# Low parts of the weights by negation and an accumulating DMA, with four buffers

## The chip, the cores and the metric

The kernel runs on one core of one Trainium2 chip. Its time is device microseconds (us) of the whole program. Names of the engines: PE is TensorE (matmuls; its weight loads are PEld), DVE is VectorE, ACT is ScalarE, POOL is GpSimd, SP is SyncE, which here issues most of the DMAs. L254 is line 254 of the kernel file.

## The reference

A trunk of two decoder layers over 512 tokens of width 1024 in float32. Per layer, with all products in full precision:

```
h = RMSNorm(x);  z = h @ W_in           # 5888 columns: attention q,k,v; retention q,k,v,g; two gates
A = sliding-window attention (window 128, 8 query and 2 key heads of 64, rotary, sinks)
B = retention (4 heads, 128 and 256 wide), normed per head, times silu(g)
y = sigmoid(gate_a) * (A @ W_a) + sigmoid(gate_b) * (B @ W_b)
x = x + y @ W_out                        # up to here: "the mixer"
x = x + relu(RMSNorm(x) @ W_up)^2 @ W_down   # "the MLP", 4096 wide
```

A last RMSNorm ends it.

## The kernel before

**Full precision out of three products.** PE multiplies in a float32 form with a shortened mantissa (float32r). Each operand is therefore split in two parts: the high part is the operand rounded to that form, the low part is what the rounding left over. A product is then high x high + high x low + low x high. These are the three matmuls of `products` on L299, L300 and L301; in the wide pairs of the MLP the two lines L1155 and L1156 do the same on 512 and 256 columns.

**Weight units.** The weights lie in HBM cut into units of 128 partitions x 1024 words (512 KB), in the order in which they are used. A layer's mixer has 66: 46 of w_in, 4 of w_a, 8 of w_b and 8 of w_out, with the w_a and w_b units standing between those of w_in. The MLP's units (w_up, w_down, and "pair" units that are sums of weight blocks) follow. `order` holds this list for both layers.

**Load, split, use.** Three functions move along that list, each with its own counter:

- `load_until` lets SP load a unit into a raw tile (L194); there are three raw tiles.
- `split_until(n)` splits all units before n: ACT rounds the raw tile into `hi` (L253; for the first half unit DVE does, L251), and DVE subtracts `hi` from the raw tile into `lo` (L254). Before each unit it calls `load_until(i + 3)`. The tiles `hi` and `lo` come from `wpool`, three buffers each, so the high part of a unit waits until PE is done with the unit three before it. The first three units are split in two halves, to start early.
- `unit` hands the next unit to PE's code and has the units up to two further on split ahead (`split_until(i + 3)`).

In the MLP `add_part` has DVE add or subtract weight blocks ahead of the split; the last units of all go to other tiles (`homes`).

**Users.** `group` uses four units for four 128-column outputs at once (five PSUM banks serve all of this), `chunk` one unit for one output of 128 columns, with two steps of background work (`advance`) between; `values` uses four units as the moving operand. A unit of the mixer is eight blocks of 128x128 and so 24 matmuls of 512 columns. Attention and retention are generators whose matmuls are put between those of the chunks.

**Order.** The order of the instructions on each engine comes from a scheduler that plans the program ahead with times of its own; each engine then runs its list strictly in order and waits where an operand isn't there. POOL has almost nothing to do before the change: constants and a few memsets at the start, one memset per layer (L545), and one scaling at the end (L506).

Of the kernel before, what the change touches and what calls it, by code (L numbers as in the profile page):

```python
# [12 lines left out]
F32R = mybir.dt.float32r  # L13
AF = mybir.ActivationFunctionType
ALU = mybir.AluOpType
# [3 lines left out]
P = 128  # L19
# [26 lines left out]
UNIT = 1024  # L46
# [9 lines left out]
def unit_order():  # L56

    order = [("w_in", i) for i in range(4 + 2 + 8 + 2 + 4 + 2)]
    order += [("w_in", i) for i in range(22, 26)]
    order += [("w_a", i) for i in range(4)]  # L60
    order += [("w_in", i) for i in range(26, 42)]
    order += [("w_b", i) for i in range(4)]
    order += [("w_in", i) for i in range(42, 46)]
    order += [("w_b", i) for i in range(4, 8)]
    order += [("w_out", i) for i in range(8)]
    for what, q, i in mlp_sequence():
        if what == "first":
            order += [("w_up", u) for u in range(4)]
        elif what == "pair":
            order += [("pair", 8 * q + 2 * i, part) for part in range(4)]  # L70
        elif what == "down":
            order += [("w_down", 8 * q + 2 * i + u) for u in range(2)]
        else:
            order += [("w_down", 8 * q + u) for u in range(8)]
    return order
# [13 lines left out]
def wide(chunk):  # L89

    return FIRST_WIDE <= chunk < LAST_WIDE
# [32 lines left out]
def decoder(ctx, tc, xT, x_first, w_in, w_a, w_b, w_out, w_up, w_down, tables, decay, band, triangles, g_last, out):  # L124
    nc = tc.nc
    weights = {"w_in": w_in, "w_a": w_a, "w_b": w_b, "w_out": w_out, "w_up": w_up, "w_down": w_down}

    const = ctx.enter_context(tc.tile_pool(name="const", bufs=1))
    wpool = ctx.enter_context(tc.tile_pool(name="wpool", bufs=3))
# [6 lines left out]
    def f32(ap):  # L136
        return ap.bitcast(F32)
# [26 lines left out]
    order = [(layer, *u) for layer in range(DEPTH) for u in unit_order()]  # L164
    raws, parts, homes = {}, {}, []
    state = {"next": 0, "loaded": 0, "split": 0}

    def halves(i):

        return (slice(0, UNIT // 2), slice(UNIT // 2, UNIT)) if i < 3 else (slice(0, UNIT),)  # L170

    last_low = []
# [11 lines left out]
    def load_until(n):  # L184
        while state["loaded"] < min(n, len(order)):
            i = state["loaded"]
            layer, name, j = order[i][:3]
            if name == "pair":
                load_part(i)
            else:  # L190
                raws[i] = raw_tile()
                for at in halves(i):
                    queue = nc.scalar if i == 0 and at.start == 0 else nc.sync
                    queue.dma_start(raws[i][:, at], weights[name][layer, j][:, at])  # L194
                    if i < 3:
                        load_x()
            state["loaded"] += 1
# [17 lines left out]
    def add_part(i):  # L215
        part = order[i][3]
        if part == 0:
            w2 = raws[i + 3]
            nc.vector.tensor_tensor(raws[i][:, RIGHT], w2[:, RIGHT], w2[:, LEFT], ALU.add)
        elif part == 1:  # L220
            w1 = raws[i - 1]
            nc.vector.tensor_tensor(raws[i][:, LEFT], w1[:, RIGHT], w1[:, LEFT], ALU.subtract)
        elif part == 2:
            raws[i] = big("raw3").rearrange("p a t -> p (a t)")
            w1, w2, z2 = raws[i - 2], raws[i + 1], raws[i - 1]
            nc.vector.tensor_tensor(raws[i][:, LEFT], w1[:, LEFT], w2[:, RIGHT], ALU.subtract)
            nc.vector.tensor_tensor(raws[i][:, RIGHT], z2[:, RIGHT], z2[:, LEFT], ALU.subtract)

    def split_until(n):
        while state["split"] < min(n, len(order)):  # L230
            i = state["split"]
            load_until(i + 3)
            paired = order[i][1] == "pair"
            if paired:
                add_part(i)
            raw = raws[i]
            if homes and i >= len(order) - len(homes):
                home = homes[len(order) - 1 - i]
                hi, lo = (home[:, 2 * a : 2 * a + 2, :].rearrange("p a t -> p (a t)") for a in range(2))
            else:  # L240


                first = (ASIDE, ASIDE) if paired else (0, 0)
                if paired and wide(order[i][2]):
                    first = (ASIDE, 0)
                hi, lo = (
                    wpool.tile([P, UNIT + P], F32R, tag=n, name=n)[:, a : a + UNIT] for n, a in zip(("hi", "lo"), first)
                )
            for at in (LEFT,) if paired and order[i][3] == 3 else halves(i):
                if i == 0 and at.start == 0:  # L250
                    nc.vector.tensor_copy(hi[:, at], raw[:, at])  # L251
                else:
                    nc.scalar.activation(hi[:, at], raw[:, at], AF.Copy)  # L253
                last_low[:] = [nc.vector.tensor_tensor(lo[:, at], raw[:, at], f32(hi[:, at]), ALU.subtract).ins]  # L254
            raws.pop(i - 3 if paired else i, None)
            parts[i] = (hi, lo)
            state["split"] += 1

    def unit(name, layer):
        i = state["next"]  # L260
        assert order[i][:2] == (layer, name), (order[i], layer, name)
        state["next"] += 1
        split_until(i + 3)
        return parts.pop(i)


# [66 lines left out]
    def chunk(name, layer, moving, evacuate, rate=1.0):  # L333

        hi, lo = unit(name, layer)
        n = len(moving)
        ps = bank(ps_mm, "mm")
        pairs = [((hi[:, k * P : (k + 1) * P], lo[:, k * P : (k + 1) * P]), moving[k]) for k in range(n)]
        advance(rate)
        products(ps, pairs[: n // 2], True, False)  # L340
        advance(rate)
        products(ps, pairs[n // 2 :], False, True)
        evacuate(ps)

    def group(name, layer, moving, evacuates, meanwhile=None):


        banks = [bank(ps_mm, "mm") for _ in range(4)]
        for u in range(4):
            hi, lo = unit(name, layer)  # L350
            for j in range(2):
                k = 2 * u + j
                for c, ps in enumerate(banks):
                    cols = slice(j * T + c * P, j * T + (c + 1) * P)
                    products(ps, [((hi[:, cols], lo[:, cols]), moving[k])], k == 0, k == KD - 1)
            if meanwhile and u in meanwhile:
                meanwhile[u]()
        return [partial(evacuate, ps) for ps, evacuate in zip(banks, evacuates)]
# [5 lines left out]
    def two_chunks(name, layer, moving, evacuates):  # L364

        banks = [bank(ps_mm, "mm") for _ in range(2)]
        for u in range(2):
            hi, lo = unit(name, layer)
            for j in range(4):
                k = 4 * u + j  # L370
                for c, ps in enumerate(banks):
                    cols = slice((2 * j + c) * P, (2 * j + c + 1) * P)
                    products(ps, [((hi[:, cols], lo[:, cols]), moving[k])], k == 0, k == KD - 1)
        for ps, evacuate in zip(banks, evacuates):
            evacuate(ps)
# [58 lines left out]
    def end(layer, uT):  # L434
# [24 lines left out]
        for u in range(4):  # L459
            weights = unit("w_down", layer)  # L460
            split_until(state["next"] + 2 + u)
            for j in range(2):
                k = 2 * u + j
                for b, ps in enumerate(banks):
                    multiply(ps, k, b, weights, k == 0, k == KD - 1)
# [803 lines left out]

    scaled_input(0, 0)  # L1270
    split_until(1)
    for u in (2, 3):
        for k in (2 * u - 3, 2 * u - 2):
# [160 lines left out]
```

## Time and profile before

| | |
|---|---|
| median of 3 runs | 1481.8 us (1481.06 to 1482.15) |
| span of the profiled execution, first to last instruction | 1480.1 us |
| the profiled execution's own time | not listed apart; the median of the runs lies 1.7 us above the span |
| DMA | 155.57 MB moved, 147.51 MB read from HBM |

The page of the profile gives busy time per engine, its share in 40 slices of the span, the DMA queues, the chain of work that ended last, and groups of equal instructions by line. A group names what is written and read (`lo<-raw,hi`), the shape, the count, the busy time in us and the mean of one in ns, and then the idle time ahead of these instructions with what ended it. A PE row's length is that of one matmul from start to end; matmuls overlap, so the pace is the distance between two starts.

### The profile page before, as it was taken

To read this page: it belongs to the slowest core of one execution; us is meant where nothing else is said; L and a number is where in the kernel's file an instruction comes from. 1 tells how busy PE (TensorE), PEld (TensorE's weight loads), DVE (VectorE), ACT (ScalarE), POOL (GpSimd) and SP (SyncE) were. 2 spreads that over 40 slices of the span, in tenths; PEclk is the share of its full clock that TensorE was granted. 3 is DMA by queue.
4 is the path that set the end of the run, shared out by engine and by line. 5 is a ranking of instruction groups with operands and counts; after the bars stand their busy time and mean duration, and the time that the engine had idled before them with its cause. 6 is when DMAs were issued, how large, how long until landed. Compare 5 with 4: busy or idle time off the path is not lost.

```text
span 1480.1 us, 18928 instructions
## 1 busy us (share of the span) xinstructions
PE 1473.5 (100%) x7106; PEld 1240.8 (84%) x7106; DVE 1097.6 (74%) x1786; ACT 765.1 (52%) x1212; POOL 3.7 (0%) x14
## 2 busy tenths in 40 slices
PE   9999999999999999999999999999999999999998
PEld 7888888888888888888888888888888888888887
DVE  7998668764688787777678975786648877787763
ACT  6656355642555445444455743556327554444553
POOL 0000000000000000000000000000000000000000
PEclk9999999999999999999999999999999999999999
DMA  6422322234323332334443233232443233333341
GB/s 225 132 90 86 93 82 89 74 126 128 100 72 114 100 114 88 107 91 130 162 128 94 86 99 87 87 100 76 128 119 102 80 99 91 108 115 110 91 141 58
DMA packets 51980, 155.57 MB, mean 105 GB/s; under 512 B 6320, under 2 KB 6448, under 8 KB 51888
## 3 DMA queue, kind: packets, MB, share of 16 engines
q1 hardware_dynamic: 51600, 153.83, 34.2%
q8 instruction: 56, 0.92, 0.3%
q10 hardware_dynamic: 288, 0.52, 0.1%
q14 instruction: 36, 0.29, 0.1%
HBM read 147.51 MB, written 4.19 MB: 102 GB/s over the span
## 4 chain that ended last, share of the span: by engine, by line
PE 100%; POOLq 0%; DVE 0%; ACT 0%; issue 0%; ACTq 0%
PE mm L299 24%; PE mm L300 24%; PE mm L301 24%; PE mm L1155 11%; PE mm L1156 6%; PE rv L299 2%; PE rv L301 2%; PE rv L300 2%; PE score L696 1%; PE r L299 1%; PE r L301 1%; PE r L300 1%; PE pT L651 0%; PE pv L677 0%; PE pv L678 0%; PE warm L278 0%
## 5 line engine op out<-in xcount | busy, mean ns | idle before, releaser
L253 ACT ACTIVATE hi<-raw 128x1024 fp32r<-128x1024 f32 (+1 forms) x314 | 316.9, 1014 | 435.2 <-PE mm L300 241.0
L254 DVE TENSOR_TENSOR lo<-raw,hi 128x1024 fp32r<-128x1024 f32 (+1 forms) x315 | 365.4, 1164 | 155.6 <-ACT hi L253 154.9
L300 PE MATMUL mm<-r,hi 128*128 128x512 f32 (+1 forms) x704 | 270.8, 385 | 0.0
L299 PE MATMUL mm<-xhl,hi 128*128 128x512 f32 (+1 forms) x696 | 268.6, 388 | 0.0
L300 PE MATMUL mm<-xhl,hi 128*128 128x512 f32 (+1 forms) x696 | 268.4, 388 | 0.0
L299 PE MATMUL mm<-r,hi 128*128 128x512 f32 (+1 forms) x704 | 268.2, 385 | 0.0
L301 PE MATMUL mm<-xhl,lo 128*128 128x512 f32 (+1 forms) x696 | 267.1, 388 | 0.0
L301 PE MATMUL mm<-r,lo 128*128 128x512 f32 (+1 forms) x704 | 266.3, 384 | 0.0
L301 PEld LDWEIGHTS mm<-r,lo 128*128 128x128 f32 x704 | 132.2, 188 | 26.7
L300 PEld LDWEIGHTS mm<-r,hi 128*128 128x128 f32 x704 | 132.2, 188 | 25.6
L299 PEld LDWEIGHTS mm<-r,hi 128*128 128x128 f32 x704 | 131.7, 188 | 26.0 <-DVE z L1134 0.2
L299 PEld LDWEIGHTS mm<-xhl,hi 128*128 128x128 f32 x696 | 131.1, 188 | 26.0 <-ACT xhl L309 0.7
L301 PEld LDWEIGHTS mm<-xhl,lo 128*128 128x128 f32 x696 | 130.8, 188 | 24.8
L300 PEld LDWEIGHTS mm<-xhl,hi 128*128 128x128 f32 x696 | 130.8, 188 | 24.6
L1155 PE MATMUL mm<-r,hi 128*128 128x512 f32 x416 | 146.7, 391 | 0.0
L1156 PE MATMUL mm<-r,lo 128*128 128x256 f32 x416 | 115.3, 277 | 0.0
L1155 PE MATMUL mm<-xhl,hi 128*128 128x512 f32 x312 | 110.4, 391 | 0.0
L1155 PEld LDWEIGHTS mm<-r,hi 128*128 128x128 f32 x416 | 78.1, 188 | 16.2
L1156 PE MATMUL mm<-xhl,lo 128*128 128x256 f32 x312 | 86.6, 277 | 0.0
L1156 PEld LDWEIGHTS mm<-r,lo 128*128 128x128 f32 x416 | 78.1, 188 | 1.8
L1155 PEld LDWEIGHTS mm<-xhl,hi 128*128 128x128 f32 x312 | 58.6, 188 | 11.9
L1156 PEld LDWEIGHTS mm<-xhl,lo 128*128 128x128 f32 x312 | 58.6, 188 | 1.7
(256 smaller groups left out, 2077.1 us busy)
## 6 DMA issues: line engine op xcount, KB each, us to landing
raw<-w_in_in SPq DMA_DIRECT2D x89, 512.0 KB, 3.6
raw<-w_down_in SPq DMA_DIRECT2D x64, 512.0 KB, 3.6
raw<-w_up_in SPq DMA_DIRECT2D x36, 512.0 KB, 3.6
raw<-w_up_in SPq DMA_DIRECT2D x56, 256.0 KB, 2.8
raw<-w_b_in SPq DMA_DIRECT2D x16, 512.0 KB, 3.6
raw<-w_out_in SPq DMA_DIRECT2D x16, 512.0 KB, 3.8
raw<-w_a_in SPq DMA_DIRECT2D x8, 512.0 KB, 3.6
x<-xT_in SPq DMA_DIRECT2D x15, 256.0 KB, 3.7
```

The source lines that it names most:

```text
L253: nc.scalar.activation(hi[:, at], raw[:, at], AF.Copy)
L254: last_low[:] = [nc.vector.tensor_tensor(lo[:, at], raw[:, at], f32(hi[:, at]), ALU.subtract).ins]
L299: nc.tensor.matmul(ps, ah, bh, start=start and i == 0, stop=False, **more)
L300: nc.tensor.matmul(ps, ah, bl, start=False, stop=False, **more)
L301: nc.tensor.matmul(ps, al, bh, start=False, stop=stop and i == n - 1, **more)
L696: nc.tensor.matmul(ps[:, g * w : (g + 1) * w], q_s[g][:, c, at], part[:, keys], start=i == 0, stop=i == 1)
L1155: nc.tensor.matmul(both, hi[:, c], m, start=start and k == 0, stop=False, **more)
L1156: nc.tensor.matmul(ps[:, :H], lo[:, c], m[:, 0, :], start=False, stop=k == 3 and start, **more)
```

## The change

For all units of w_in, w_a, w_b and w_out from the fourth of the program on, the low part is made in another way: DVE multiplies the high part by -1 into `lo`, and then a DMA issued by GpSimd reads the unit from HBM once more and adds it to what stands in `lo`. ACT's rounding stays, and so does SP's load of the raw tile. The MLP's units are split as before. The tiles `hi` and `lo` get four buffers instead of three, for all units, and `unit` splits one unit further ahead. The scratch memory for the descriptors of GpSimd's DMAs is set to 4096 bytes.

```diff
@@ split_until @@
-                    wpool.tile([P, UNIT + P], F32R, tag=n, name=n)[:, a : a + UNIT] for n, a in zip(("hi", "lo"), first)
+                    wpool.tile([P, UNIT + P], F32R, tag=n, name=n, bufs=4)[:, a : a + UNIT] for n, a in zip(("hi", "lo"), first)
                 )
+            if i >= 3 and order[i][1] in ("w_in", "w_a", "w_b", "w_out"):
+                nc.scalar.activation(hi, raw, AF.Copy)
+                last_low[:] = [nc.vector.tensor_scalar(lo, f32(hi), -1.0, None, ALU.mult).ins]
+                nc.gpsimd.dma_start(lo, weights[order[i][1]][order[i][0], order[i][2]], accum_op=ALU.add)
+                raws.pop(i)
+                parts[i] = (hi, lo)
+                state["split"] += 1
+                continue
@@ unit @@
-        split_until(i + 3)
+        split_until(i + 4)
@@ kernel @@
-    nc = bacc.Bacc("TRN2", target_bir_lowering=False, num_devices=1)
+    nc = bacc.Bacc("TRN2", target_bir_lowering=False, num_devices=1, dynamic_dma_scratch_size=4096)
```

In the changed kernel the new lines are L250 (rounding), L251 (negation) and L252 (the DMA); lines behind them stand eight further on (L299 becomes L307).

## The prediction

> **What bounds the kernel now.** The page's head, engine shares and slices come first: they tell whether any engine other than the busiest can matter at all.
>
> ```profile
> span 1480.1 us, 18928 instructions
> PE 1473.5 (100%) x7106; PEld 1240.8 (84%) x7106; DVE 1097.6 (74%) x1786; ACT 765.1 (52%) x1212; POOL 3.7 (0%) x14
> ...
> PE   9999999999999999999999999999999999999998
> ...
> PEclk9999999999999999999999999999999999999999
> DMA  6422322234323332334443233232443233333341
> ```
>
> TensorE (PE) is busy in every slice at full granted clock. A busy PE need not run at its peak, so the next view is busy time by stretches; each row gives a stretch, its length, busy time per engine, clock, DMA share and GB/s.
>
> ```profile
> 0.00:35.00 35.00, 33.93 (x137) 27.39 (x138) 25.11 (x34) 25.76 (x41) 1.93 (x12) 1.00 0.69 228
> 35.00:170.00 135.00, 135.00 (x644) 112.83 (x642) 116.78 (x269) 81.23 (x164) 0.00 (x0) 1.00 0.34 99
> 170.00:330.00 160.00, 160.00 (x739) 134.13 (x738) 115.86 (x169) 80.71 (x116) 0.00 (x0) 1.00 0.31 94
> 1170.00:1480.00 310.00, 304.61 (x1561) 259.29 (x1559) 223.55 (x349) 152.11 (x241) 0.83 (x1) 1.00 0.33 102
> ```
>
> PE idles 1.07 us (35.00 - 33.93) at the start and 5.39 us (310.00 - 304.61) at the end, and nowhere between; 1480.1 - 1473.5 = 6.6 leaves nothing for other stretches. The chain of waits shows the pace.
>
> ```profile
> 314.33 0.91 PE mm L299 x4
> ...
> 1474.70 0.48 ACT sq L492 x2
> 1475.83 0.87 POOLq L1429
> ```
>
> Four matmuls of 512 columns take 0.91 us, 0.2275 each. A weight unit of the mixer (128x1024, eight 128-column blocks, three products each) is 24 of them: 24 x 0.2275 = 5.46 us. The end is ACT and POOL finishing the last rows, work that the change leaves alone. So the bound is PE's own work. VectorE's (DVE's) 74% costs nothing: PE nowhere waits for it, nor for the low parts. **Freeing DVE can therefore bring nothing, and the question is only whether the new way is ever late.**
>
> **The change part by part.** It concerns 129 units: layer 0 has 46 + 4 + 8 + 8 = 66 of w_in, w_a, w_b and w_out, less the first three, and layer 1 all 66.
>
> *Subtraction becomes negation.* The groups, kept apart by shape, give the old price (busy us, mean ns), the answer on one line the nearest negation (min/median/max ns).
>
> ```profile
> L254 DVE TENSOR_TENSOR lo<-raw,hi 128x1024 fp32r<-128x1024 f32 x281 | 343.2, 1222 | 152.6 <-ACT hi L253 151.9
> L253 ACT ACTIVATE hi<-raw 128x1024 fp32r<-128x1024 f32 x281 | 297.7, 1060 | 429.1 <-PE mm L300 239.2 <-PE mm L1155 83.3 <-issue 75.1
> L254 DVE TENSOR_TENSOR lo<-raw,hi 128x512 fp32r<-128x512 f32 x34 | 23.3, 686 | 3.0 <-ACT hi L253 3.0
> ...
> L584 DVE TENSOR_SCALAR r<-klo,x x4: 477/480/484, 44.4 to 768.6; 128x512 fp32r<-128x512 f32 x4
> ```
>
> Twice the elements cost the subtraction 1222 - 686 = 536 ns more, so 150 ns of 686 are fixed. A negation of 512 columns at 480 has 330 moving; of 1024 it is 150 + 660 = 810 ns (an estimate; at most the subtraction's 1222, at least 480). DVE loses 129 x (1.22 - 0.81) = 53 us of busy time, all beside PE's matmuls: **0**.
>
> *The accumulating DMA.* The trace has no DMA from GpSimd and none that adds. It reads the unit from HBM a second time, reads the negated tile, and writes it. Nearest rows: KB each and median us to landing, the queue's share of 16 engines, and the DMA's fastest stretch.
>
> ```profile
> q1 hardware_dynamic: 51600, 153.83, 34.2%
> ...
> raw<-w_in_in SPq DMA_DIRECT2D x89, 512.0 KB, 3.6
> raw<-w_up_in SPq DMA_DIRECT2D x56, 256.0 KB, 2.8
> r<-qlo SPq DMA_DIRECT2D x32, 64.0 KB, 2.4
> raw<-w_in_in SPq DMA_DIRECT2D x5, 256.0 KB, 5.7
> ```
>
> ```profile
> 8.00:10.00 2.00, 2.00 (x11) 1.65 (x10) 2.00 (x4) 2.00 (x5) 0.00 (x0) 1.00 1.06 406
> ```
>
> From 64 to 512 KB a landing grows by 1.2 us for 448 KB: 1.37 us move 512 KB and 2.2 are fixed. Lower bound: a plain load, 3.6. Upper: three transfers one after the other, 10.8, and GpSimd's longest instruction on top for writing the transfer out:
>
> ```profile
> 0.90 0.95 POOL L545 MEMSET r<- 128x1024 f32 x1
> ```
>
> That makes 11.8. I take two streams, because two reads meet in one write: 2.2 + 2 x 1.37 + 0.95 = **5.9 us** alone. The nearest row, the plain load, supports the lower half.
>
> The Trainium skill says the same of the add: in "Collectives: The Full Stack", section "The bandwidth ceiling: the fold count and why AG ≠ RS ≠ AR", an adding transfer runs at half a copy's rate because of its two source reads, the add itself costing nothing. No transfer here can show it; by that rule the 5.9 stands, and with a free second read it would be 4.5.
>
> *The lead in the steady mixer, and the fourth buffer.* In the first stretch below ACT makes one high part per unit and DVE follows.
>
> ```profile
> 335.50 1.06 ACT L253 ACTIVATE hi<-raw 128x1024 fp32r<-128x1024 f32 x1 [3.86 <-issue]
> 340.94 1.06 ACT L253 ACTIVATE hi<-raw 128x1024 fp32r<-128x1024 f32 x1 [3.86 <-issue]
> ...
> 336.60 1.23 DVE L254 TENSOR_TENSOR lo<-raw,hi 128x1024 fp32r<-128x1024 f32 x1 [0.23 <-ACT hi L253]
> ```
>
> The step is 5.44 us, one unit. With three buffers a high part begins when the unit three back is done, so two units (10.9) lie before its use; less 336.60 + 1.23 - 335.50 = 2.33, a low part is ready some 8.6 us early. A fourth buffer and the wider lookahead add 5.46, the shorter negation 0.41: **14.5 us** for the DMA, against 5.9 alone and 11.8 at worst. Cost 0; were the cover gone, each unit would be late by a quarter of the excess, since four buffers share one round. Queued behind a waiting DMA on POOL are only the next units' DMAs, layer 1's value-tile memset and the last scaling; SP's queue and its loads are not behind it. The high part alone now frees a raw tile, so loads can start earlier.
>
> *DMA capacity.* At 406 GB/s 512 KB take 1.29 us of all engines; by the queue row (34.2% of 1480.1 us for 153.83 MB) 1.73. Load plus two-read accumulate is 3.9 to 5.2 us per unit, under 5.46: no cost, but no wide margin.
>
> *The first units.* Here the lead is short. Unit 3 is the first with the new way.
>
> ```profile
> 16.62 1.05 ACT L253 ACTIVATE hi<-raw 128x1024 fp32r<-128x1024 f32 x1
> ...
> 18.83 1.21 DVE L254 TENSOR_TENSOR lo<-raw,hi 128x1024 fp32r<-128x1024 f32 x1
> ...
> 20.69 1.23 DVE L254 TENSOR_TENSOR lo<-raw,hi 128x1024 fp32r<-128x1024 f32 x1
> ...
> 22.67 0.39 PE L299 MATMUL mm<-xhl,hi 128*128 128x512 f32 x1
> ...
> 24.48 1.07 PE L301 MATMUL mm<-xhl,lo 128*128 128x512 f32 x4
> ```
>
> Unit 3's matmuls begin at 22.67, and its low part is first used at 24.48, after 8 others. In the compiled order of the changed kernel 11 stand ahead (two of unit 4 and the square sum's were pulled in): 22.67 + 11 x 0.2275 = 25.17. The negation ends at 18.83 + 0.81 = 19.64. That leaves 5.5 us. The DMA queues are not empty then:
>
> ```profile
> 18.00:20.00 2.00, 2.00 (x11) 1.65 (x10) 2.00 (x4) 1.04 (x2) 0.00 (x0) 1.00 0.55 225
> 20.00:24.00 4.00, 4.00 (x19) 3.33 (x18) 2.76 (x5) 2.35 (x3) 0.00 (x0) 1.00 0.67 201
> ```
>
> With the queues full, the first loads of 256 KB took 5.7 instead of 2.8, twice. Fully doubled, the moving part makes 2.2 + 5.5 + 0.95 = 8.7; at a share near 0.6 I take the middle of 5.9 and 8.7, 7.3. PE then stands 7.3 - 5.5 = **1.8 us** (bounds: 0 at 3.6, 6.3 at 11.8). Unit 4 is negated by 20.69 + 0.81 = 21.5 and first used 27 matmuls after 22.67, at 28.8 plus the stall: 9.1 us, enough; later units have more.
>
> *Moved order.* The wider lookahead and fourth buffer hold in the MLP too, where split and load stay as they are. PE's compiled order changes there, mostly by early first matmuls of a pair. Until now nothing idles in it, so the change can only lose; I take 0, at most 2 us, the first units' size.
>
> *Sum:* 0 + 0 + 0 + 1.8 = 1.8 on the span, 1481.9. The profiled execution's own time is its span and what lies around it; the median of the runs shown, 1481.8, is 1.7 above the span, and I carry that over: 1481.8 + 1.8 = **1483.6 us**.
>
> **The rivals.**
>
> *A, the DMA engines become the bound (slower).* Place: the mixer. It decides once an accumulate occupies the engines for more than 5.46 - 1.29 = 4.17 us, 3.2 copies (2.2 copies by the 1.73). Price at four copies: 5 x 1.29 = 6.45 us per unit. The mixers run to about 406 us in layer 0, 6.2 per unit with attention and retention between, so 129 x (6.45 - 6.2) = 32 us, 1514. For it: the adding is unmeasured and the margin thin. Against: DMA is at 0.31 to 0.34 in these stretches, and four buffers smooth bursts. Chance 0.18.
>
> *B, negation and descriptor writing shut each other out (slower).* If GpSimd can't write a transfer's descriptors while DVE runs a negation, unit 3's transfer waits behind the negations of units 4, 5 and 6, which follow closely at the start (18.83, 20.69): 3 x 0.81 = 2.4 more, 1486.0; in the steady mixer 0.8 disappears in 14.5. The row for it: 480 ns against 686 shows a faster mode for one source. Against: no instruction of POOL lies beside one here. Chance 0.05.
> The Trainium skill has that rule in "SBUF — State Buffer", section "Who interferes with whom": an fp32 single-source operation between SBUF tiles can take the port pair that GpSimd writes descriptors through, for the whole instruction. The 480 ns fit such a mode; no run here shows the lock.
>
> *C, the relief speeds something (faster).* It would have to shorten PE's idle time at the two ends, 1.07 + 5.39 = 6.5 us, of which the change touches neither; half of it would give 1478.5. PE's pace is even and its clock full, so there is nothing else to speed. Chance 0.02.
>
> *D, the change doesn't do what it says:* the extra buffer moves the order, and the MLP loses about 2 us while the start hides: 1483.8. Chance 0.04, three parts of it within 0.2%.
>
> **How the numbers follow.** 0.2% is 2.96 us, about what a measurement of this kernel tells from no change: 1478.8 to 1484.8. The forecast, a start-only stall, has 0.71; its own range is 1481.8 + 0 to + 6.3, less the 1.1 between the runs shown (1481.06 to 1482.15): 1480.7 to 1488.1. Stalls up to 3.0 (a transfer of at most 8.5 us at the start) get 0.50 of it, longer ones 0.21. Same: 0.50 + 0.03 = 0.53. Slower: 0.21 + 0.18 + 0.05 + 0.01 = 0.45. Faster: 0.02. The range reaches from 1480.7 to 1490.0, the upper bound of the start with D's 2 us; A and C, 0.20 together, are left out.
>
> **What would show it.** Right: the group of matmuls on the changed lines keeps 0.2275 each; PE's busy time is unchanged, with one gap of 1 to 3 us near 25 us, released by a DMA into lo; negations near 810 ns, DVE busy near 1045; accumulates landing in 5 to 8 us; HBM read 129 x 0.524 = 68 MB more; DMA share about 0.6 to 0.9 in the mixer. Wrong: gaps on PE spread through the mixer (A), landings over 14.5 us, a start without any gap (transfer under 5.5), or a first GpSimd transfer that takes far longer than later ones, which no row here bounds.

## The result, and the profile after

The changed kernel takes **1491.0 us** (median of 4 runs, 1489.27 to 1492.68) against 1481.7 (1481.06 to 1482.15). The ratio is 1.0064, 95% interval [1.0049, 1.0078]: 9.4 us slower. Forecast were 1483.6 us and a range up to 1490.0. The profiled execution took 1490.64 us, with a span of 1488.9 (before: 1480.1).

The page of the kernel after, head, shares, slices, queues and HBM:

```profile
span 1488.9 us, 19181 instructions
PE 1477.0 (99%) x7106; PEld 1242.2 (83%) x7106; DVE 1030.3 (69%) x1786; ACT 766.2 (51%) x1212; POOL 116.1 (8%) x143
...
PE   8999999999999999999999999999999999999998
...
DMA  9977877799723332334698788777995232333341
...
q1 hardware_dynamic: 51600, 153.83, 32.5%
q0 software_dynamic: 18576, 67.64, 27.6%
...
HBM read 215.15 MB, written 4.19 MB: 147 GB/s over the span
```

PE is still busy everywhere but in the first slice. The DMA engines, at 2 to 4 tenths before, stand at 7 to 9 in both mixers. q0 is the new queue: 27.6% of 1488.9 us for 129 units is 3.18 us of all engines per adding transfer; q1 gives 32.5% of 1488.9 for 293.4 loads' worth of 512 KB (153.83 / 0.5243), 1.65 each.

Busy time by stretches of the kernel after (stretch, length, PE, PEld, DVE, ACT, POOL, clock, DMA share, GB/s), first the start and the mixer of layer 0, then the start looked at closely:

```profile
0.00:35.00 35.00, 29.03 (x107) 23.01 (x108) 23.39 (x34) 21.24 (x34) 5.94 (x16) 0.90 0.89 274
35.00:170.00 135.00, 135.00 (x639) 112.51 (x638) 101.67 (x264) 84.00 (x167) 18.76 (x22) 1.00 0.82 184
170.00:330.00 160.00, 160.00 (x741) 134.27 (x740) 104.42 (x170) 80.84 (x117) 21.27 (x26) 1.00 0.80 172
```

```profile
24.00:29.00 5.00, 0.47 (x3) 0.04 (x1) 4.30 (x3) 0.69 (x1) 0.92 (x2) 0.92 1.01 253
29.00:35.00 6.00, 5.87 (x14) 4.60 (x15) 1.47 (x3) 1.78 (x3) 0.00 (x0) 0.50 1.05 275
35.00:40.00 5.00, 5.00 (x24) 4.12 (x23) 3.45 (x7) 4.52 (x7) 0.86 (x1) 1.00 0.84 208
```

From 35 us on PE waits once more, 0.3 us for ACT near the end (1460 us). The waiting lies before: PE stands from 24.5 to 29.1, and **from 29 to 35 it has half its clock**, 14 matmuls in 6 us instead of the 28 of the kernel before. PE's own rows show both (start, length, idle time before and what ended it):

```profile
24.08 0.39 PE L413 MATMUL ssq<-sh,ones 128*128 128x512 f32 x1
29.13 2.07 PE L309 MATMUL mm<-xhl,lo 128*128 128x512 f32 x4 [4.67 <-DMA lo<-w_in_in]
31.00 0.63 PE L307 MATMUL mm<-xhl,hi 128*128 128x512 f32 x1
31.43 0.63 PE L308 MATMUL mm<-xhl,hi 128*128 128x512 f32 x1
...
34.84 0.48 PE L307 MATMUL mm<-xhl,hi 128*128 128x512 f32 x1
```

The distance of two starts is 0.43 where it was 0.2275, for some 13 matmuls: 13 x 0.20 = 2.6 us. Summing over the starts of all matmuls how far each lies behind that even pace, the 160 matmuls from 13 to 49 us carry 7.7 us after and none before. The rest lies in the MLPs, in pieces of 0.1 to 0.5: the stretch from 1145 us to the last matmul has 3.2 instead of 2.2. PE's last matmul starts 8.7 us later, 1482.99 instead of 1474.33.

POOL's rows of the kernel after show the transfer that PE waited for and the three behind it; of the two answers on landing, one is for the first transfer, the other for all four:

```profile
19.87 1.03 POOL L252 DMA_DIRECT2D lo<-w_in_in  x1 [17.21 <-DVE lo L251]
21.74 1.25 POOL L252 DMA_DIRECT2D lo<-w_in_in  x1 [0.84 <-DVE lo L251]
23.19 0.86 POOL L252 DMA_DIRECT2D lo<-w_in_in  x1 [0.21 <-issue]
24.86 0.87 POOL L252 DMA_DIRECT2D lo<-w_in_in  x1 [0.81 <-DVE lo L251]
```

```profile
DMA to landing us min/median/max: 9.2/9.2/9.2
...
DMA to landing us min/median/max: 9.2/12.3/15.4
```

One by one the four land after 9.2, 11.1, 13.5 and 15.4 us: each is later than the one before it.

The groups and the median landings of the kernel after:

```profile
L251 DVE TENSOR_SCALAR lo<-hi 128x1024 fp32r<-128x1024 f32 x129 | 89.0, 690 | 97.8 <-ACT hi L250 97.5
L252 POOL DMA_DIRECT2D lo<-w_in_in x89 | 77.6, 872 | 527.3 <-DVE lo L251 313.1
```

```profile
lo<-w_in_in POOLq DMA_DIRECT2D x89, 512.0 KB, 6.7
...
r<-qlo SPq DMA_DIRECT2D x32, 64.0 KB, 4.8
```

The last row is one that the change doesn't touch: SP's 64 KB transfers of the attention's low parts took 2.4 before.

### The profile page after: what moved, and what is told of

The parts are those of the page before. It is cut to its first block, busy times and chain, and to the rows that moved or that the text cites. A ratio compares the mean times of both kernels' runs of the same rounds, so it can differ in the third digit from the quotient of the medians.

```text
span 1488.9 us, 19181 instructions
## 1 busy us (share of the span) xinstructions
PE 1477.0 (99%) x7106; PEld 1242.2 (83%) x7106; DVE 1030.3 (69%) x1786; ACT 766.2 (51%) x1212; POOL 116.1 (8%) x143
## 3 DMA queue, kind: packets, MB, share of 16 engines
q1 hardware_dynamic: 51600, 153.83, 32.5%
q0 software_dynamic: 18576, 67.64, 27.6%
## 4 chain that ended last, share of the span: by engine, by line
PE 97%; DMA 1%; DVE 1%; issue 0%; ACT 0%; SPq 0%; POOLq 0%; DVEq 0%; ACTq 0%
PE mm L309 23%; PE mm L307 23%; PE mm L308 23%; PE mm L1163 11%; PE mm L1164 6%; PE rv L307 2%; PE rv L308 2%; PE rv L309 2%; PE score L704 1%; DMA lo<-w_in_in 1%; PE r L307 1%; PE r L309 1%; PE r L308 1%; PE pT L659 0%; PE pv L685 0%; PE pv L686 0%
## 5 line engine op out<-in xcount | busy, mean ns | idle before, releaser
L261 ACT ACTIVATE hi<-raw 128x1024 fp32r<-128x1024 f32 (+1 forms) x185 | 178.5, 980 | 209.9 <-DVE raw L219 65.8
L307 PE MATMUL mm<-xhl,hi 128*128 128x512 f32 (+1 forms) x696 | 269.6, 389 | 0.3 <-ACT xhl L317 0.3
L307 PE MATMUL mm<-r,hi 128*128 128x512 f32 (+1 forms) x704 | 268.1, 385 | 0.0
L262 DVE TENSOR_TENSOR lo<-raw,hi 128x1024 fp32r<-128x1024 f32 (+1 forms) x186 | 206.7, 1123 | 57.1 <-ACT hi L261 56.6
L250 ACT ACTIVATE hi<-raw 128x1024 fp32r<-128x1024 f32 x129 | 136.6, 1059 | 210.4 <-PE mm L308 137.1
L309 PEld LDWEIGHTS mm<-xhl,lo 128*128 128x128 f32 x696 | 131.6, 189 | 30.3 <-DMA lo<-w_in_in 5.1
L251 DVE TENSOR_SCALAR lo<-hi 128x1024 fp32r<-128x1024 f32 x129 | 89.0, 690 | 97.8 <-ACT hi L250 97.5
L307 PEld LDWEIGHTS mm<-r,hi 128*128 128x128 f32 x704 | 132.0, 188 | 26.2
L307 PEld LDWEIGHTS mm<-xhl,hi 128*128 128x128 f32 x696 | 131.3, 189 | 25.5 <-ACT xhl L317 0.7
L308 PEld LDWEIGHTS mm<-xhl,hi 128*128 128x128 f32 x696 | 131.3, 189 | 24.8
L309 PEld LDWEIGHTS mm<-r,lo 128*128 128x128 f32 x704 | 130.7, 188 | 25.4
L252 POOL DMA_DIRECT2D lo<-w_in_in x89 | 77.6, 872 | 527.3 <-DVE lo L251 313.1
```

The costliest lines, as they stand in the source:

```text
L250: nc.scalar.activation(hi, raw, AF.Copy)
L251: last_low[:] = [nc.vector.tensor_scalar(lo, f32(hi), -1.0, None, ALU.mult).ins]
L252: nc.gpsimd.dma_start(lo, weights[order[i][1]][order[i][0], order[i][2]], accum_op=ALU.add)
L307: nc.tensor.matmul(ps, ah, bh, start=start and i == 0, stop=False, **more)
L308: nc.tensor.matmul(ps, ah, bl, start=False, stop=False, **more)
L309: nc.tensor.matmul(ps, al, bh, start=False, stop=stop and i == n - 1, **more)
```

## The experiments

The theories, as the expectations name them: S, the start's stop and the slow clock behind it carry the loss; L, the load on the DMA engines carries it; O, the changed order carries part of it; Q, the small transfers of `qlo` come late; B, the lock of the second rival. Each run stood beside runs of the kernel before, medians 1481.2 to 1481.6.

### Which units carry the loss

**The first four units alone:**

```diff
-            if i >= 3 and order[i][1] in ("w_in", "w_a", "w_b", "w_out"):
+            if 3 <= i < 7 and order[i][1] in ("w_in", "w_a", "w_b", "w_out"):
```

> The new way for units 3 to 6 of the first group and chunks only (4 of 129); all later units are split as before; four buffers and the wider lookahead stay. Theory S (start): the whole loss is one stop of TensorE at unit 3's low part (about 4.7 us of idle) and its half clock for about 5.7 us after it (13 matmuls at 0.43 in place of 0.23, 2.6 us); so 1489 to 1492 us, like the changed kernel, with the same gap near 24 us. Theory L (load): 125 more accumulating DMAs keep the DMA engines busy through both mixers and cost there; then at most half the loss is left, 1482 to 1486. Theory O (order): the fourth buffer and the moved order in the MLP cost; then this too keeps its part whatever the start does.

Measured: 1489.7 us, ratio 1.0056 [1.0044, 1.0069]. This run loses 8.5 of the 9.4 us; 2.1 of them are the order's (below), so 6.4 are those of the four units. PE waits 3.2 us in the profiled execution; the stretch behind, in this run:

```profile
29.00:35.00 6.00, 6.00 (x17) 4.64 (x16) 2.86 (x4) 2.37 (x4) 0.00 (x0) 0.57 1.05 276
```

17 matmuls in 6 us, at a clock of 0.57: stop and slow clock both come from these four units.

**All but those four:**

```diff
+            if i >= 7 and order[i][1] in ("w_in", "w_a", "w_b", "w_out"):
```

> The new way only from unit 7 on (125 of 129 units); units 3 to 6 are subtracted as before. Theory S: no gap at the start, everything later is hidden: 1480.5 to 1483 us, within 0.2% of before, and the DMA engines as busy in the mixer (0.8) as in the changed kernel. Theory L: 1486 to 1491. Theory O: 1483 to 1486, wherever the order costs.

Measured: 1487.3 us, ratio 1.0043 [1.0031, 1.0056], 4 us above the expectation of S and inside that of L. The stop at 25 us is gone, and others that the kernel after doesn't have come instead. The first line of PE's waits in this run (in all, times, longest), and the row of the longest one:

```profile
PE score L701 <- DMA r<-qlo: 1.7, 2, 1.5
```

```profile
65.75 0.36 PE L701 MATMUL score<-r,r 128*128 128x256 f32 x1 [1.48 <-DMA r<-qlo]
```

Attention's score matmuls wait for the 64 KB transfers, landing again at 4.8 instead of 2.4. Two more score matmuls start late without a releaser that the profile shows; by their starts the four are 3.0 us late in all, of the 4.0 that this run lies above the one with the buffers alone (1483.3, below). The last 1 us is not assigned. In the kernel after the small transfers land as late, but there PE has already lost 7 us at 25. The two losses do not add: less the order's 2.1, the 6.4 us of the first four units and the 4.0 of the rest make 7.3 together. My reading, which no run shows, is that the first 60 us are short of DMA, and that whichever wait comes first pays for the next. The next run speaks against the second half of it: useless matmuls hold PE up nearly as long there, and the score matmuls wait all the same.

**The stop filled with useless work.** 24 matmuls into a bank that nobody reads stand ahead of unit 3's products:

```diff
+            if state["next"] == 4:
+                more = bank(ps_aux, "more")
+                for _ in range(24):
+                    nc.tensor.matmul(more, hi[:, :P], xh[:, 0, :], start=True, stop=True)
```

> The changed kernel with 24 matmuls more, whose result nobody reads, in the place of the gap ahead of unit 3's first low part (24 x 0.2275 = 5.46 us of work). If the slow matmuls after the gap are the clock falling because TensorE stood idle (theory S), they are gone: the loss is 5.5 to 6 us, 1487 to 1488 us, and the granted clock after 29 us reads 1.0. If they come from something else at that time (the busy DMA engines, theory L, or SBUF traffic), matmuls after 29 us stay at 0.43 us and the time is 1490 or more.

Measured: 1493.1 us, ratio 1.0082 [1.0068, 1.0095]. The same two stretches in this run:

```profile
24.00:29.00 5.00, 5.00 (x24) 4.14 (x23) 3.39 (x3) 0.69 (x1) 1.02 (x2) 1.00 1.02 253
29.00:35.00 6.00, 6.00 (x28) 4.99 (x27) 3.05 (x4) 3.00 (x6) 0.00 (x0) 1.00 1.05 276
```

With PE kept busy, the DMA share as high as in the kernel after, the clock stays at 1.00 and 28 matmuls fit where 14 did. That shows the cause of the slow matmuls: PE's own pause, not the DMA traffic. The time didn't fall to the expected 1487 or 1488. The expectation held the 5.5 us of the useless work, but not the order's 2.1 us, and not the waits that this run has elsewhere: of the score matmuls 1.5 us for `qlo` and 1.2 for ACT, of another matmul 0.8 for ACT. Together that is 1492.3; about 1 us is not assigned.

**None of the first units: from column unit 14 of w_in on.**

```diff
+            if order[i][1] in ("w_a", "w_b", "w_out") or (order[i][1] == "w_in" and order[i][2] >= 14):
```

> The new way for w_a, w_b, w_out and for the units of w_in from the 15th of each layer on; the first 14 of each layer are subtracted. 102 of 129 accumulating DMAs remain, but none lies beside the first group or beside the small transfers of the attention's queries (landing 2.4 us before, 4.8 us in the changed kernel). Theory Q (what was left in the run from unit 7 on were TensorE's score matmuls, late because those small transfers share busy DMA engines): no gap is left in either mixer, and the time is that of the buffers alone, 1482.8 to 1484 us. Theory L (125 accumulates cost a little everywhere): 1485.5 to 1487, in proportion.

Measured: 1483.3 us (11 runs), ratio 1.0012 [1.0003, 1.0021]. Layer 0 makes its units from 14 on in the new way, and so does layer 1: 104 of the 129 (the expectation's 102 is a miscount). PE waits for no low part and no `qlo` in either mixer; `qlo` lands at 2.3 again. **104 adding transfers cost nothing**; theory Q holds, and the 1.6 us that are left are no more than the 2.1 of the next run.

### The order

**No low part in the new way, only the four buffers, the lookahead and the descriptor memory:**

```diff
-            if i >= 3 and order[i][1] in ("w_in", "w_a", "w_b", "w_out"):
+            if False:
```

> Only the fourth buffer, the wider lookahead and the smaller scratch; every low part is subtracted as before. Theory S: within 0.2% of before, 1481 to 1483 us (the even pace of TensorE leaves nothing to gain, the order of the MLP moves by at most 2). Theory O: 1484 or more, and the same extra gaps in the MLP and at the end as in the changed kernel.

Measured: 1483.3 us (11 runs), ratio 1.0013 [1.0005, 1.0022]: 2.1 us, between the two expectations.

**The wider lookahead kept out of the MLP**, on top of the run from unit 14 on:

```diff
-        split_until(i + 4)
+        split_until(i + (4 if name in ("w_in", "w_a", "w_b", "w_out") else 3))
```

> The low parts are made in the new way from column unit 14 on, as in the run with 1483.25 us, and the four buffers stay, but the wider lookahead (four units instead of three) is kept to w_in, w_a, w_b and w_out; the MLP looks three units ahead as before. Theory O (the 1.6 to 2.1 us that remain when nothing waits come from PE's changed order in the MLP, which the wider lookahead moves): 1481.2 to 1482.0, and the idle time of PE's last stretch (1170 us to the end) back from 6.4 to about 5.4. Rival (they come from the low parts themselves, or from the fourth buffer): 1483 to 1484 as before.

Measured: 1483.4 us (11 runs), ratio 1.0013 [1.0004, 1.0021]. Theory O in that form falls.

**The fourth buffer alone**, in the kernel before (with the smaller descriptor memory, which makes room for it; the run with three buffers and the same memory, below, keeps the order of before at the place shown here, so the memory doesn't move it):

```diff
-                    wpool.tile([P, UNIT + P], F32R, tag=n, name=n)[:, a : a + UNIT] for n, a in zip(("hi", "lo"), first)
+                    wpool.tile([P, UNIT + P], F32R, tag=n, name=n, bufs=4)[:, a : a + UNIT] for n, a in zip(("hi", "lo"), first)
```

> The kernel before with one thing changed: four buffers for the high and low parts (and the smaller descriptor memory, which makes room for them). Lookahead and low parts as before. Theory F (the fourth buffer moves the planned order, at the end of the last MLP above all): 1483 to 1483.5, with the 0.3 us wait of PE for ACT at 1452 us. Rival G (the wider lookahead in the mixer does it): 1481.2 to 1482.

Measured: 1483.1 us (11 runs), ratio 1.0013 [1.0004, 1.0022]: 1.8 us, and the loss is whole with the fourth buffer alone. Its largest piece, in this run's rows of PE:

```profile
1452.12 1.25 PE L447 MATMUL xT<-ident,x 128*128 128x128 f32 x10
1453.69 0.50 PE L299 MATMUL mm<-r,r 128*128 128x512 f32 x1 [0.31 <-ACT mm L473]
```

The planned order has ten of the last transposes at this place, and PE waits for ACT behind them; before, one stood there and nothing waited. The rest are small pieces in the MLPs, as where a weight load waits for DVE's low part (this run, then the kernel before at the place above):

```profile
526.55 0.19 PEld L1156 LDWEIGHTS mm<-xhl,lo 128*128 128x128 f32 x1 [0.26 <-DVE lo L254]
```

```profile
1451.27 0.27 PE L447 MATMUL xT<-ident,x 128*128 128x128 f32 x1
```

**The wider lookahead alone, with three buffers**, in the kernel before:

```diff
-        split_until(i + 3)
+        split_until(i + 4)
```

> The kernel before with one thing changed: the wider lookahead, with three buffers. Theory F: 1481.2 to 1482.2, as before. Rival G: 1483 to 1483.5.

Measured: 1484.7 us (11 runs), ratio 1.0022 [1.0013, 1.0031]. That is above both expectations. This run's waits:

```profile
PE mm L301 <- DVE lo L254: 2.3, 2, 1.2
```

PE waits 1.15 us for a subtraction near 446 us and again near 1180, at the head of each MLP. The run with both has no such wait: that loss goes with the fourth buffer, whose own 1.8 us stay.

### Is the lead needed?

**From unit 14 on, but with three buffers and the old lookahead:**

```diff
-                    wpool.tile([P, UNIT + P], F32R, tag=n, name=n, bufs=4)[:, a : a + UNIT] for n, a in zip(("hi", "lo"), first)
+                    wpool.tile([P, UNIT + P], F32R, tag=n, name=n, bufs=3)[:, a : a + UNIT] for n, a in zip(("hi", "lo"), first)
-        split_until(i + 4)
+        split_until(i + 3)
```

> As the run before, but with three buffers and the old lookahead. If the moved order of the MLP is what four buffers cost (theory O, 2.1 us), that cost is gone. By the leads of the trace of before (8.6 us in the steady mixer, measured landings 6.7 to 7.2 from the issue), most units are still hidden; units with a short lead (25: 4.1, 21: 4.5, 22: 5.7 us in layer 0) must be late by 2 to 3 us each: gaps there, 2 to 8 us in all, 1483 to 1489 us. If the fourth buffer wasn't needed at all: 1481 to 1482.

Measured: 1490.9 us (5 runs, 1489.9 to 1496.0), ratio 1.0064 [1.0050, 1.0078], 1.9 us above the expected range. The waits of PE and, around the longest, three stretches of the traced execution, the longest of the five with 1495.95 us:

```profile
PE mm L309 <- DMA lo<-w_in_in: 5.6, 4, 1.8
PE rv L308 <- DMA lo<-w_in_in: 3.4, 1, 3.4
...
PE mm L309 <- DMA lo<-w_out_in: 0.3, 1, 0.3
```

```profile
155.00:164.00 9.00, 9.00 (x43) 7.60 (x42) 2.22 (x4) 3.18 (x3) 2.24 (x2) 1.00 0.64 142
164.00:167.50 3.50, 0.30 (x3) 0.10 (x1) 0.75 (x2) 0.00 (x0) 0.86 (x1) 0.91 1.05 238
167.50:174.00 6.50, 6.34 (x16) 4.98 (x17) 0.52 (x1) 0.72 (x2) 0.00 (x0) 0.52 0.65 159
```

The fourth buffer and the wider lookahead, taken together, are needed: with the short lead six waits come, and the one of 3.4 us again leaves some 6 us at half clock, 140 us away from the start. The fall is not a matter of the start.

### What the transfer is made of

**Unit 3 alone in the new way:**

```diff
+            if i == 3:
```

> The new way for unit 3 alone; all other units subtract. It asks what made unit 3's transfer take 9.2 us at the start, where 7.3 were forecast. Theory S1 (the loads that are under way at that time): a landing of 8 to 9 us, PE waits 3.5 to 4.5 us for it, and the slow matmuls follow: 1487.5 to 1489.5. Rival S2 (the three adding transfers behind it, which share the engines): a landing of 6 to 7.5 us, a wait of 1.5 to 3 us with no slow matmuls behind it: 1484.5 to 1486.5. Both hold some 2 us of the changed order.

Measured: 1484.4 us (10 runs), ratio 1.0019 [1.0010, 1.0028]. The issue, its landing and PE's wait:

```profile
L252 POOL DMA_DIRECT2D lo<-w_in_in x1: 1029/1029/1029, 20.6 to 20.6; - x1
...
DMA to landing us min/median/max: 8.5/8.5/8.5
```

```profile
26.68 0.39 PE L308 MATMUL mm<-xhl,hi 128*128 128x512 f32 x1
29.08 1.20 PE L309 MATMUL mm<-xhl,lo 128*128 128x512 f32 x4 [2.02 <-DMA lo<-w_in_in]
```

S1 is right on the landing: 8.5 us with no adding transfer behind it, where the median of all of them in the kernel after is 6.8 and the shortest 5.3; so SP's loads make it slow, and the three behind it add at most some 0.7. There is more loading at this place than before, too. The first row is the kernel before, the second the run from unit 14 on, which has the four buffers, the wider lookahead and at this time no adding transfer yet:

```profile
24.00:29.00 5.00, 5.00 (x23) 4.13 (x22) 1.31 (x2) 2.67 (x5) 0.00 (x0) 1.00 0.61 210
24.00:29.00 5.00, 5.00 (x23) 4.13 (x22) 1.23 (x1) 4.13 (x7) 0.00 (x0) 1.00 0.86 313
```

The share rises from 0.61 to 0.86 by loads that run further ahead. S2 is right on the wait and, within 0.1 us, on the time, for another reason: in this order PE comes to the low part later, at 26.68 + 0.39 = 27.07, and leaves 6.4 us from the issue at 20.6. No slow matmuls follow the 2.0 us.

**A plain transfer in place of the adding one.** The split is left out here: the low part becomes the weight itself.

```diff
-                nc.gpsimd.dma_start(lo, weights[order[i][1]][order[i][0], order[i][2]], accum_op=ALU.add)
+                nc.gpsimd.dma_start(lo, weights[order[i][1]][order[i][0], order[i][2]])
```

> The changed kernel with GpSimd's DMA writing the unit over the negated part in place of adding to it (one read and one write, no add; the low part is then the weight itself, so the split is left out). If the second read is half of the accumulate's price (estimate: 1.37 us more to move, and twice that at a busy start), unit 3's transfer lands in 6.5 to 7.5 us instead of 9.2, the gap is 2 to 3 us instead of 4.7, and the GpSimd queue's share falls from 27.6% to about 14%: 1484 to 1488 us. If the gap were GpSimd's own path (writing the transfer out), landing and gap stay: 1490 to 1492.

Measured: 1488.6 us (4 runs), ratio 1.0047 [1.0033, 1.0061]. Its queue and median landing:

```profile
q0 software_dynamic: 18576, 67.64, 15.5%
...
lo<-w_in_in POOLq DMA_DIRECT2D x89, 512.0 KB, 4.7
```

15.5% of 1484.9 us over 129 units is 1.78 us of all engines, against 3.18 with the add; the landing is 4.7 instead of 6.7. So the adding costs a second stream, as the prediction took it. The first transfer lands after 7.8 us, above the expected 6.5 to 7.5, and PE still waits 2.8 us for it in the profiled execution. The four times lie in pairs, 1486.7 and 1487.1 with a mean clock of 1.000, 1490.4 and 1490.1 with 0.996. Only the first was traced; that a stop near 3 us keeps the clock in one execution and loses it in the next is what the clocks suggest.

**The negation on ACT**, so that no VectorE instruction is behind the first transfers:

```diff
-                last_low[:] = [nc.vector.tensor_scalar(lo, f32(hi), -1.0, None, ALU.mult).ins]
+                last_low[:] = [nc.scalar.activation(lo, f32(hi), AF.Copy, scale=-1.0).ins]
```

> The changed kernel with the negation on ScalarE (a copy scaled by -1) in place of VectorE. In the changed kernel GpSimd's DMA instructions take 0.86 us, but 1.03 and 1.25 where a negation on VectorE runs inside them. Rival B (negation and the writing out of a transfer shut each other out): all take 0.86 now, and the first transfer lands up to 0.4 us after a shorter time from its issue. Otherwise the long ones stay. Time within 2 us of the changed kernel in both cases, as ScalarE makes a unit's two parts one after the other.

Measured: 1490.0 us (one run). POOL's first rows:

```profile
18.79 1.03 POOL L252 DMA_DIRECT2D lo<-w_in_in  x1 [16.15 <-DVE acc L392]
23.09 1.78 POOL L252 DMA_DIRECT2D lo<-w_in_in  x2 [3.26 <-ACT lo L251]
26.05 0.87 POOL L252 DMA_DIRECT2D lo<-w_in_in  x1 [1.18 <-ACT lo L251]
```

The first instruction takes 1.03 us as with the negation on DVE; the second and third 0.89 each instead of 1.25 and 0.86. A lock could hold at most those 0.4 us; the first landing is 8.8 instead of 9.2. Theory B fails as a cause: it priced 2.4 us. PE's stop is 3.0 us here, as the transfer is issued 1.1 us earlier (18.79 against 19.87), and the clock stays at 1.00. Behind it comes another stop, for unit 4's transfer:

```profile
33.18 0.50 PE L309 MATMUL mm<-xhl,lo 128*128 128x512 f32 x1 [1.03 <-DMA lo<-w_in_in]
```

### How much room the DMA engines have

**A second adding transfer of 768 columns per unit**, useless work into a spare tile, from unit 14 on:

```diff
+                nc.gpsimd.dma_start(spare, weights[order[i][1]][order[i][0], order[i][2]][:, : spare.shape[1]], accum_op=ALU.add)
```

> The new way from column unit 14 on, and with every adding transfer a second one of 768 of the 1024 columns into a spare tile that nobody reads: useless work, to find where the DMA engines become the bound. By the queue's share an adding transfer of 512 KB holds all engines for 3.2 us and a load for 1.65, so a unit now needs 1.65 + 1.75 x 3.2 = 7.2 us of them against 5.46 us of PE's matmuls. Load theory: DMA share at 1.0 between 80 and 400 us, landings above 12 us, PE waits for low parts all through the mixer, in all 20 to 100 us more. Rival (most of an adding transfer's time is waiting that others can fill): share below 1.0, below 10 us more.

Measured: 1727.8 us, ratio 1.165 [1.1626, 1.1673], 246 us lost, more than either theory gave, at a share of 0.77 to 0.86 in the mixer of layer 0. It doesn't decide. The group of the second transfers in this run shows why:

```profile
L255 POOL DMA_DIRECT2D spare<-w_in_in x64 | 57.6, 900 | 303.5 <-DMA spare<-w_in_in 266.7
```

All of them write one tile, so each waits on POOL for the one before it to land, 267 us in all, and the next unit's low part is queued behind it.

**Two of 256 columns each, into three tiles in turn:**

```diff
+                for p in range(2):
+                    at = slice((2 * i + p) % 3 * 256, (2 * i + p) % 3 * 256 + 256)
+                    nc.gpsimd.dma_start(spare[:, at], weights[order[i][1]][order[i][0], order[i][2]][:, at], accum_op=ALU.add)
```

> The new way from column unit 14 on, and for every such unit two more adding transfers of 256 columns each into a spare tile's three parts in turn: useless work, half an adding transfer more per unit, without the chain of the run with 768 columns. Engines per unit: 1.65 + 1.5 x 3.2 = 6.4 us, against 5.46 us where only matmuls of weights run and 6.2 on the mixer's average. Load theory: share at 1.0 in the mixer and 10 to 60 us more, landings above 10 us. Rival (the loss of 246 us came from the chain of waits alone): below 5 us more than the run without them (1483.25).

Measured: 1604.1 us, ratio 1.0837 [1.0817, 1.0856]. Two stretches of this run:

```profile
35.00:170.00 135.00, 107.34 (x468) 86.71 (x466) 93.99 (x245) 68.20 (x146) 73.49 (x82) 0.89 0.91 176
170.00:330.00 160.00, 127.58 (x508) 102.57 (x509) 62.03 (x100) 51.34 (x75) 87.52 (x99) 0.88 0.97 185
```

The share is 0.91 to 0.97, PE idles a fifth of the time, and the clock falls with it (0.88). The load theory has the direction and nearly the share; its 10 to 60 us are half of the 121 measured, and its landings above 10 us didn't come (the low parts' median is 7.2). How much of the loss is the engines', how much the half clock after each stop, and how much the waits on POOL that are left (its spare transfers still wait 181 us in all for one another), was not told apart. For the change itself it bounds the room: half an adding transfer, 1.6 us, more on the 6.2 us per unit would take the share of 0.80 to 1.06 (an estimate), so less than that is left.

## Why the prediction was wrong, point by point

- **The bound: right.** PE's pace sets the time wherever nothing is late; DVE's relief of 67 us busy brought nothing.
- **The negation: right.** 690 ns instead of 810, cost 0.
- **The adding transfer: right in kind.** It costs two streams: 3.18 us of the engines against 1.78 plain, 1.79 times. Its median landing, beside loads, is 6.7 us against 5.9 estimated alone; none ran alone here. POOL needs 0.86 us for it, 0.95 were taken. The Trainium skill's rule ("Collectives: The Full Stack", section "The bandwidth ceiling: the fold count and why AG ≠ RS ≠ AR"), stated there for the reducing step of a collective, says half a copy's rate; the trace agrees in kind, with 1.8 times instead of 2.
- **The lead in the steady mixer: right.** From unit 14 on no transfer was late with four buffers and the wider lookahead; with three buffers and the old one, six were.
- **DMA capacity: right as a sum, not as a whole.** 1.65 + 3.18 = 4.83 us per unit lies in the forecast's 3.9 to 5.2, and the first rival didn't come. But the step asked only after the weights. Traffic at this share also doubles the landing of the 64 KB transfers, 2.4 to 4.8, and where PE isn't already late, attention waits for them: in the run from unit 7 on, 3.0 of the 4.0 us (1487.3 less the order's 1483.3) are late score matmuls.
- **The first units: this is the step that failed.** It read: "at a share near 0.6 I take the middle of 5.9 and 8.7, 7.3. PE then stands 7.3 - 5.5 = 1.8 us". The landing was 9.2 us, 1.9 more. The share of 0.6 was read at 18 to 24 us, but more than half of the transfer's time lies behind: from 24 to 29 us the share was 1.01, to which loads that run further ahead (0.86 without any adding transfer) and the new transfers both add. The window was 4.6 us, not 5.5, as PE came earlier (24.08 + 0.39 = 24.47 is the end of its last matmul; 24.47 - 19.87 = 4.6). 9.2 - 4.6 = 4.6 us of stop, inside the step's bounds of 0 to 6.3. What no bound held is what follows a stop: the half clock, 2.6 us. Together 7.3 us instead of 1.8.
- The same step had unit 4 at "9.1 us, enough; later units have more". Of the next three transfers each landed later than the one before, 11.1 to 15.4 us, the last past the 14.5 that the prediction had named as a sign of being wrong. Unit 4's, issued at 21.74, landed at 32.8, some 2 us after the 30.6 at which the forecast had its first use (28.8 plus the stop of 1.8). In the kernel after PE came later still, so nothing shows; with the negation on ACT it was the second stop, 1.03 us.
- The pace of that half clock could have been read in the trace of before, though the clock column reads 1.00 there. Ahead of the first product stand ten `warm` matmuls in 4.64 us, 0.46 each, twice as long as later:

```profile
1.04 4.64 PE L278 MATMUL warm<-ones 128*128 128x512 f32 x10 [1.04 <-DVE ones L273]
```

- For such a clock the Trainium skill states a rule in "TensorE: Matmul & The Clock Gate", section "Part 1: The HAM clock gate (the "warmup" mystery)": about 3.4 us of idle time halve PE's clock, and it takes as long a busy time to come back. The runs here: stops of 2.0, 2.8 and 3.0 us kept the clock in the profiled executions, stops of 3.2, 3.4 and 4.7 lost it. The way back took longer than the rule's, 5.7 us (29.13 to 34.84 in the kernel after, 28.48 to 34.19 in the run with the first four units).
- **Moved order: forecast 0, at most 2; measured 1.8 with the fourth buffer alone**, 2.1 with the wider lookahead too.
- **The signs it named**: HBM read 67.6 MB more (forecast 68), the share of 0.80 to 0.87 in the mixer of layer 0 and DVE's 1030 us (near 1045) came. PE's busy time rose by 3.5 us instead of staying, 2.6 of it in the matmuls at half clock.
- **The sum**: 1.8 (order) + 7.3 (start) = 9.1 of the 9.4 us. 0.3 are not assigned. The chances put 0.21 on a start longer than 3.0 us; the range ended 1.0 us too low, since its upper end held the order's 2 us and the longest stop, but no slow clock.
- **The rivals**: A did not come, by the share of 0.80 and the run from unit 14 on, though the room is small; B holds at most 0.4 us; C did not come; D's order came with its price, beside the start and not in its place.

No version here beats the kernel before: PE has no idle time that a lighter DVE could give back.

## What to carry to other kernels

Where one engine sets the pace, look for the first use of a new, slower way, when queues are full and no lead has been built up: four units of 129 cost 6.4 us here and the 104 from unit 14 of each layer on nothing, while the other 21 cost some 4 where the start was left as it had been. Price a stop of TensorE by what follows it as well: here a pause of 4.7 us cost another 2.6 us at half clock. And before putting more traffic on the DMA engines, list the small transfers that others wait for; here their landing doubled at a share of 0.8.

## What the runs showed of the hardware that was not expected

- In the traced executions PE's clock was at half after pauses of 3.2, 3.4 and 4.7 us and stayed there for about 5.7 us of dense matmuls; after 2.0, 2.8 and 3.0 us, and with 24 useless matmuls in the pause, it was not. In the run with plain transfers, the same kernel took 3.3 us longer in two of four executions, with a mean clock of 0.996 instead of 1.000.
- The 64 KB transfers, on another queue than the adding ones, took 4.8 us instead of 2.4 at a mean DMA share of 0.8, and 3.9 beside plain transfers of the same bytes.
- GpSimd's instruction takes 0.86 us for an adding transfer of 512 KB and 0.53 for a plain one; the first of a run took longer, 1.03 and 0.71.
- Half an adding transfer more per unit turned a kernel that lost 1.6 us into one that lost 123, part of it by transfers that waited on POOL for one another.
